# The five written-out queue orders of a one-core hybrid decoder layer, exchanged for another set

## The chip, the cores and the metric

The kernel runs on one core of a Trainium2 chip. The metric is the device time of one execution in microseconds (us), taken as the median of several runs. The core has five instruction queues that matter here: PE (TensorE, the matmuls), DVE (VectorE), ACT (ScalarE), POOL (GpSimd) and SP (SyncE, which only issues transfers; ACT issues some too). Each queue is served in the order in which its instructions stand, and an instruction whose data are not there holds up everything behind it on its queue.

## The reference

One layer of a decoder over 2048 prompt tokens and 8 single-token samples, in 32-bit floats, with width 1024:

```python
xn = _rmsnorm(x, norm1_g)
z = jnp.einsum('btd,de->bte', xn, w_in)
xr, gr, q, k, v = jnp.split(z, IN_SPLITS, axis=-1)
xc, new_conv = _causal_conv(xr, conv_buf, conv_w, conv_b)
hs, h_last = _rglru(xc, h0, gate_a_w, gate_a_b, gate_x_w, gate_x_b, lru_lambda)
rec = (hs * jax.nn.gelu(gr.astype(jnp.float32))).astype(x.dtype)
att = _prompt_attention(q, k, v, attn_sinks)   # window 128, with a sink per head
...
mix = jnp.concatenate([_rmsnorm(rec, rec_norm_g), _rmsnorm(att, attn_norm_g)], axis=-1)
h = x + jnp.einsum('bte,ed->btd', mix, w_out)
hn = _rmsnorm(h, norm2_g)
ff = jax.nn.silu(jnp.einsum('btd,df->btf', hn, w_gate)) * jnp.einsum('btd,df->btf', hn, w_up)
y = h + jnp.einsum('btf,fd->btd', ff, w_down)
```

The inner width of the last part (the FFN) is 2816. The samples use caches of keys and values, and the caches, shifted by one, are outputs too.

## The kernel before

**Numbers in two parts.** Every value that goes into a matmul is split in a high part (a CAST to a shorter 32-bit form, `fp32r`) and a low part (the value minus the high part), and every product is three matmuls: high by high, high by low, low by high (`mm3`, L990). So each weight tile that comes from memory, such as `raw_in` for the input projection, is cast on ACT to a high half (L936), its low half is made on POOL or DVE (L937), and the pair is stored for later use (`split_w`, L955).

**Stages.** Tokens go through the input projection (matmuls `ip`), the recurrence (`rec_chunk`, L1320), the attention (`attn_item`, L1484) and the output projection (`out_unit` and `out_half`, L1623 and L1652) in four groups of 520, 512, 512 and 512 tokens. The FFN then takes three portions of 344 or 342 token columns at a time by two. It uses the seven products of a fast 2x2 block multiplication in place of eight, so the blocks are first added and subtracted: `hn_mix` (L1070) loads parts of the normed stream (`n<-hs`), combines them on DVE (L1082, L1090) and stores the combinations (`mixed<-n`); `hn_load` (L1127) fetches them (`m<-mixed`) and splits them to high and low (ACT L1138; DVE or POOL L1139) as tiles `hn`. `products` (L1914) multiplies them by the gate weights into PSUM tiles `ps_g` and by the up weights into `ps_u`, and copies or adds the banks together in SBUF tiles `c_g` and `c_u` (ACT L1985 and L1990, DVE L1964); `down` (L2003) takes the way back (`pd`, `pw`, and DVE adds to `y`).

**Places where the prediction's steps lie.**

- At the start, 256 KB weight pieces `raw_in` (three buffers), the tokens `xs`, the gate weights `gw` and copies of the two caches (`out_skw`, `out_svw`, L1178 and L1179) all come through SP. `prep_first` (L1228) makes the normed tokens `xn` (L998, L999).
- In the attention, an exponential is turned by PE (`pt`, L968), its high half `pth` is cast on ACT (L1536), its low half `ptl` is made on DVE (L1537), and PE multiplies both by the values (`o`). The recurrence is a scan on DVE (L1376, one instruction per chunk) with two products `rrec` (L1384). `hn_mix` for the first FFN portion runs beside the last attention blocks and has few stage buffers: a load `n<-hs` waits until an older `mixed<-n` store from the same buffer has ended.
- At the entry of the FFN, `out_half` stores the last pieces of the stream from tiles `xres` (`hs<-xres`, L1688, on ACT's queue), while the first gate and up products begin.

**What sets the order.** The program is written as some hundred generators (`x0`, `r33`, `mix0` ...) which a small planner (`Chains`) interleaves. What decides in the end is the table `ORDER` at L104: for each of the five engines one string of runs, `key+pop:count`, where the key is a generator (or for PE a group of matmuls). `order` (L972) takes the instructions in that sequence and links each to the one before it with a dependency that carries no wait, so the string is the order of the queue. Waits for data and buffers are added on top and don't depend on the table.

Of the kernel before, what the change touches and what calls it, by code (L numbers as in the profile page):

```python
# [2259 lines left out]
```

## Time and profile before

| what | value |
|---|---|
| median of 3 runs | 2038.34 us (2037.39 to 2038.42) |
| the profiled execution, its time | 2035.2 us |
| the profiled execution, its span | 2033.4 us |
| PE busy | 2004.7 us (99% of the span), 12273 matmuls |
| DVE busy | 1472.9 us (72%) |
| ACT busy | 955.0 us (47%) |
| POOL busy | 906.8 us (45%) |
| mean granted TensorE clock, by 50 us | 1.00 but for the first, the last and two others |

The span is the time from the first to the last instruction of one execution; the time holds 1.8 us more that lie around it. In the windows view each row is one stretch of the span, with each engine's busy time in it and, in brackets, the number of instructions. In the timeline view a row is an instruction or a run of equal ones: start, duration, engine, line, what it writes and reads, and in square brackets how long the engine had been idle and whose work ended that. In the chain view a row is a start, a duration and what the end of the program was waiting for at that time. An engine name with a q behind it (SPq) is the queue at issue.

### The profile page before, as it was taken

What the parts mean: (1) busy time and instruction counts of PE and PEld (TensorE: products, weight loads), DVE (VectorE), ACT (ScalarE), POOL (GpSimd) and SP (SyncE); (2) the same over time, 40 slices, a digit from 0 to 9 for tenths busy, and PEclk for the clock granted to TensorE, in tenths of its full rate; (3) what the DMA queues carried; (4) which work ended last, traced back from release to release, by engine and by line L of the source; (5) the groups of instructions that cost most, each with busy time, mean ns of one, the idle gap of its engine ahead of it and who ended that gap; (6) DMA issues with size and microseconds to landing.
All of it is one profiled execution on the core that took longest, in us unless ns stands there. A gap on an engine that the chain in (4) does not pass through costs nothing.

```text
span 2033.4 us, 34750 instructions
## 1 busy us (share of the span) xinstructions
PE 2004.7 (99%) x12273; PEld 1904.5 (94%) x12273; DVE 1472.9 (72%) x2694; ACT 955.0 (47%) x1960; POOL 906.8 (45%) x799
## 2 busy tenths in 40 slices
PE   9999999999999999999999999999999999999997
PEld 8988887888778999999999999999999999999997
DVE  6888986777886777765555777787767666776675
ACT  5776764654563543443344533343335433433443
POOL 4312451120132796676666645565557422322333
PEclk9999999999999999999999999999999999999999
DMA  9863675667688776764546687776668675555552
GB/s 338 297 215 127 225 273 182 210 197 223 206 288 272 285 245 208 240 212 168 184 172 224 229 282 242 261 240 214 228 209 290 204 236 196 182 197 199 195 173 101
DMA packets 208991, 450.98 MB, mean 222 GB/s; under 512 B 25232, under 2 KB 82720, under 8 KB 208800
## 3 DMA queue, kind: packets, MB, share of 16 engines
q1 hardware_dynamic: 205184, 445.73, 65.2%
q10 hardware_dynamic: 3632, 3.02, 0.5%
q8 instruction: 97, 1.59, 0.3%
q14 instruction: 78, 0.64, 0.1%
HBM read 335.89 MB, written 113.84 MB: 221 GB/s over the span
## 4 chain that ended last, share of the span: by engine, by line
PE 88%; DMA 6%; DVE 4%; issue 1%; ACT 1%; SPq 0%; DVEq 0%; ACTq 0%
PE ps_g L963 20%; PE ps_u L963 20%; PE ip L963 14%; PE pw L963 12%; PE pd L963 11%; PE op L963 5%; PE s L963 1%; DMA m<-mixed 1%; PE g L963 1%; PE pt L968 1%; PE o L963 1%; DMA mixed<-n 1%; DMA y<-hs 1%; DMA xs<-in_xT 0%; DMA hn<-mixed 0%
## 5 line engine op out<-in xcount | busy, mean ns | idle before, releaser
L963 PE MATMUL ps_g<-hn,w_g 128*128 128x342 f32 (+1 forms) x2772 | 546.0, 320 | 1.8 <-DMA w_g<-split_g 1.0
L963 PE MATMUL ps_u<-hn,w_u 128*128 128x342 f32 (+1 forms) x2772 | 529.8, 320 | 4.5 <-ACT c_u L1985 3.5
L963 PEld LDWEIGHTS ps_u<-hn,w_u 128*128 128x128 f32 x2772 | 455.0, 189 | 5.5 <-ACT c_u L1985 3.8
L963 PEld LDWEIGHTS ps_g<-hn,w_g 128*128 128x128 f32 x2772 | 456.6, 189 | 2.5 <-ACT w_d L1778 2.3
L963 PE MATMUL ip<-xn,w_in 128*128 128x512 f32 (+1 forms) x1680 | 367.3, 361 | 3.9 <-ACT w_in L936 2.7
L963 PEld LDWEIGHTS ip<-xn,w_in 128*128 128x128 f32 x1680 | 271.5, 190 | 49.4 <-issue 4.8
L2050 DVE TENSOR_TENSOR y<-y,pw 128x342 f32<-128x342 f32 x504 | 242.7, 506 | 94.8 <-PE pw L963 90.4
L963 PE MATMUL pd<-fh,w_d 128*128 128x344 f32 (+1 forms) x960 | 235.0, 320 | 0.0
L963 PE MATMUL op<-mix,w_out 128*128 128x512 f32 (+1 forms) x960 | 209.8, 362 | 0.3 <-DVE mix L999 0.3
L2021 DVE TENSOR_TENSOR y<-y,pd 128x344 f32<-128x344 f32 (+1 forms) x240 | 119.6, 509 | 103.3 <-PE pd L963 91.1
L963 PEld LDWEIGHTS op<-mix,w_out 128*128 128x128 f32 x960 | 157.6, 190 | 30.0 <-issue 6.1
L963 PE MATMUL pw<-fh,wd 128*128 128x342 f32 x576 | 167.5, 319 | 1.0 <-DVE y L2021 1.0
L963 PEld LDWEIGHTS pd<-fh,w_d 128*128 128x128 f32 x960 | 167.3, 188 | 0.0
L963 PE MATMUL pw<-t,wd 128*128 128x342 f32 x648 | 150.6, 319 | 0.0
L963 PE MATMUL pd<-fl,w_d 128*128 128x344 f32 (+1 forms) x480 | 147.6, 320 | 0.0
L1946 POOL TENSOR_TENSOR c_u<-c_u,c_g 128x342 f32<-128x342 f32 (+1 forms) x60 | 58.8, 980 | 180.2 <-DVE c_u L1964 144.5
L1964 DVE TENSOR_TENSOR c_u<-c_u,ps_u 128x342 f32<-128x342 f32 (+1 forms) x99 | 50.5, 510 | 122.1 <-PE ps_u L963 121.8
L1935 DVE TENSOR_TENSOR fl<-c_u,fh 128x342 fp32r<-128x342 f32 (+1 forms) x132 | 118.5, 909 | 15.3 <-ACT fh L1934 14.2
L1779 POOL TENSOR_TENSOR w_u<-ru,w_u 128x512 fp32r<-128x512 f32 x44 | 58.9, 1340 | 151.8 <-ACT w_u L1778 123.0
L1934 ACT CAST fh<-c_u 128x342 fp32r<-128x342 f32 (+1 forms) x132 | 62.1, 479 | 106.4 <-POOL c_u L1946 41.9
L963 PEld LDWEIGHTS pw<-t,wd 128*128 128x128 f32 x648 | 111.4, 189 | 0.0
L963 PEld LDWEIGHTS pw<-fh,wd 128*128 128x128 f32 x576 | 105.6, 189 | 1.3 <-DVE y L2021 1.3
(299 smaller groups left out, 3499.9 us busy)
## 6 DMA issues: line engine op xcount, KB each, us to landing
w_g<-split_g SPq DMA_DIRECT2D x88, 512.0 KB, 4.4
w_u<-split_u SPq DMA_DIRECT2D x88, 512.0 KB, 5.5
w_in<-split_w SPq DMA_DIRECT2D x84, 512.0 KB, 3.6
rg<-in_wgate SPq DMA_DIRECT2D x110, 256.0 KB, 3.1
ru<-in_wup SPq DMA_DIRECT2D x110, 256.0 KB, 3.3
w_out<-split_w SPq DMA_DIRECT2D x48, 512.0 KB, 4.8
split_g<-w_g SPq DMA_DIRECT2D x44, 512.0 KB, 2.8
split_u<-w_u SPq DMA_DIRECT2D x44, 512.0 KB, 2.9
```

What stands on the lines that cost most here:

```text
L963: r = nc.tensor.matmul(*args, **kw)
L968: r = nc.tensor.transpose(*args)
L1779: lo_eng.tensor_tensor(w[:, 1, :], src, w[:, 0, :].bitcast(F32), op=ALU.subtract)
L1934: nc.scalar.copy(hi, v)
L1935: nc.vector.tensor_tensor(lo, v, hi.bitcast(F32), ALU.subtract)
L1946: (nc.vector if p == NPAIR - 1 or src is not v else eng(E_MUL[2 * h + n])).tensor_tensor(v, src, g, op=ALU.mult)
L1964: nc.vector.tensor_tensor(o, a, b, op)
L2021: nc.vector.tensor_tensor(ys[gi, n, m], ys[gi, n, m], ps, ALU.add)
L2050: nc.vector.tensor_tensor(v, v, ps, ALU.add)
```

## The change

Only the five strings of `ORDER` differ. They hold the same instructions of every engine (12043 entries for PE, 2566 for DVE, 1815 for ACT, 795 for POOL, 1416 for SP) in another order, found by a planner which takes it that VectorE and GpSimd never work at the same time. Constants, tiles, buffers, engines of each operation and waits for data stay. The table is longer by 61 lines, so every line number of the code behind it is higher by 61 (L963 becomes L1024). Core of the diff, the first line of PE's and of SP's string:

```diff
 ORDER = {
     "PE": """
-w_st_x0:17 ip0_1_0 ip0_1_1 ip0_12_1 ip0_12_0 ip0_1_0:2 ip0_1_1:2 ip0_1_0 ip0_12_1 ip0_1_1 ip0_12_0:2 ip0_12_1 ip0_12_0
+w_st_x0:17 ip0_1_0 ip0_1_1 ip0_12_1 ip0_12_0 ip0_1_1 ip0_12_1 ip0_1_1 ip0_1_0 ip0_12_0 ip0_1_0:2 ip0_1_1 ip0_12_0
...
     "SP": """
-x0:9 x0+1 x0+1 x0+1 pro+1 pro x0 r01 pro v0 q02 xs1:2 cache:2 v0+1 r01 k0 q02 k0+1 v0 r00 v0 xs1:2 r00+1 k0 r03 k0
+x0:9 x0+1 x0+1 x0 v0 x0 pro xs1 r01 v0+1 xs1 r01 cache pro+1 q02 k0 q02 k0+1 cache v0 pro r00 v0 cache r00+1 r03 xs1
```

Of the entries, 53% keep their place on PE, 30% on DVE, 47% on ACT, 63% on POOL and 37% on SP; the others move by a few places, and in the steady part of the FFN whole groups move further (the loads and sums of `hn_mix` for the second and third portion by up to 91 places on SP and 148 on DVE).

**SP, the start.** The first twelve transfers that follow the tokens, before:

```order
L1239 DMA cs<-in_cst 128x384
L1185 DMA gw<-in_gatew 128x1024
L1184 DMA scv<-in_sconv 128x96
L931 DMA raw_in_12_1_185<-in_win 128x512
L955 DMA split_w<-w_in_1_0_166 128x1024
L1186 DMA sh<-in_sh 128x32
L931 DMA raw_in_9_0_368<-in_win 128x512
L955 DMA split_w<-w_in_12_0_171 128x1024
L1292 DMA xt_0_1418<-in_xR 128x512
L1292 DMA xt_1_1421<-in_xR 128x512
L1178 DMA out_skw<-in_ck 8x16256
L1179 DMA out_svw<-in_cv 8x16256
```

and after:

```order
L992 DMA raw_in_12_1_185<-in_win 128x512
L992 DMA raw_in_9_0_368<-in_win 128x512
L1300 DMA cs<-in_cst 128x384
L1245 DMA scv<-in_sconv 128x96
L1353 DMA xt_0_1418<-in_xR 128x512
L1016 DMA split_w<-w_in_1_0_166 128x1024
L992 DMA raw_in_9_1_374<-in_win 128x512
L1353 DMA xt_1_1421<-in_xR 128x512
L1016 DMA split_w<-w_in_1_1_180 128x1024
L1239 DMA out_skw<-in_ck 8x16256
L1247 DMA sh<-in_sh 128x32
L1016 DMA split_w<-w_in_12_0_171 128x1024
```

`raw_in_9_1` stood behind all twelve of the first list, and is seventh now. Two pieces of `raw_in` go first, and `gw`, `sh`, `xt_1`, one of the two stores `split_w` and both cache copies (`out_skw`, `out_svw`) come behind `raw_in_9_1`.

**DVE, near the end of the attention.** The scans of the last recurrence chunks (`q<-..,carry,ix`), the two products `rrec`, softmax steps (`sc`), an addition to the stream (`xres`) and the three steps of `hn_mix` on tiles `n_3_0` and `n_3_1`, before:

```order
L1376 SCALAR_TENSOR_TENSOR q_1_5902<-a_2_5901,carry,ix_2_5899 128x512
L1376 SCALAR_TENSOR_TENSOR q_1_5902<-ia_3_5945,carry,ix_3_5952 128x512
L1384 SCALAR_TENSOR_TENSOR rrec<-rrec,q_1_5902 128x512 x2
L1526 TENSOR_SCALAR sc_0_6723<-sc_0_6723,mx_0_6724 128x256 x2
L1638 TENSOR_TENSOR xres_5_6137<-xres_5_6137,op_5_0_6188 128x512
L1082 SCALAR_TENSOR_TENSOR n_3_1_5510<-n_3_1_5510,vec,hb_1_5363 128x344
L1082 SCALAR_TENSOR_TENSOR n_3_0_5513<-n_3_0_5513,vec,hb_0_5356 128x344
L1090 TENSOR_TENSOR n_3_1_5510<-n_3_1_5510,n_3_0_5513 128x344
L1537 TENSOR_TENSOR ptl_1_0_6701<-pt_1_0_6695,pth_1_0_6700 128x512
```

and after:

```order
L1699 TENSOR_TENSOR xres_5_6137<-xres_5_6137,op_5_0_6188 128x512
L1143 SCALAR_TENSOR_TENSOR n_3_0_5513<-n_3_0_5513,vec,hb_0_5356 128x344
L1143 SCALAR_TENSOR_TENSOR n_3_1_5510<-n_3_1_5510,vec,hb_1_5363 128x344
L1151 TENSOR_TENSOR n_3_1_5510<-n_3_1_5510,n_3_0_5513 128x344
L1587 TENSOR_SCALAR sc_0_6723<-sc_0_6723,mx_0_6724 128x256
L1437 SCALAR_TENSOR_TENSOR q_1_5902<-ia_3_5945,carry,ix_3_5952 128x512
L1445 SCALAR_TENSOR_TENSOR rrec<-rrec,q_1_5902 128x512
L1587 TENSOR_SCALAR sc_0_6723<-sc_0_6723,mx_0_6724 128x256
L1445 SCALAR_TENSOR_TENSOR rrec<-rrec,q_1_5902 128x512
L1598 TENSOR_TENSOR ptl_1_0_6701<-pt_1_0_6695,pth_1_0_6700 128x512
```

The three `n` steps stood behind the second scan and both products; they stand ahead of them now, and the product and scan rows come behind whatever those steps wait for.

**ACT and PE, the entry of the FFN.** ACT's queue around the copy that empties the first bank of the up product (`c_u_0_10<-ps_u_0_1`), before:

```order
L1943 ACT_TABLE_LOAD
L1943 ACTIVATE c_g_0_00_7116<-c_g_0_00_7116 128x344
L1688 DMA hs<-xres_4_6798 128x512
L1138 CAST hn_1_8_7715<-m_4_0_7714 128x344
L1778 CAST w_u_0_7_7886<-s_u_0_7884 128x512
L1138 CAST hn_1_8_7715<-m_4_1_7719 128x344
L1985 COPY c_u_0_10_7130<-ps_u_0_1_7909 128x344
L1943 ACTIVATE c_g_0_11_7119<-c_g_0_11_7119 128x344
L1138 CAST hn_1_9_7720<-m_4_2_7724 128x344
```

and after:

```order
L1749 DMA hs<-xres_4_6798 128x512
L1199 CAST hn_1_8_7715<-m_4_0_7714 128x344
L1199 CAST hn_1_8_7715<-m_4_1_7719 128x344
L2004 ACT_TABLE_LOAD
L2004 ACTIVATE c_g_0_00_7116<-c_g_0_00_7116 128x344
L1839 CAST w_u_0_3_7905<-s_u_0_7903 128x512
L1199 CAST hn_1_9_7720<-m_4_2_7724 128x344
L1839 CAST w_u_0_5_7866<-s_u_0_7844 128x512
L2004 ACTIVATE c_g_0_11_7119<-c_g_0_11_7119 128x344
L2004 ACTIVATE c_g_0_01_7117<-c_g_0_01_7117 128x344
L2046 COPY c_u_0_10_7130<-ps_u_0_1_7909 128x344
```

The store `hs<-xres_4` was behind a load of a function table and one activation, and is ahead of both now; the copy to `c_u_0_10`, which was fourth behind that store, is tenth now. On PE, the last rows ahead of the first matmuls of `w_u_0_6`, which write the bank that this copy empties, and these themselves, before:

```order
L963 MATMUL ps_g_0_1_7771<-hn_1_8_7715,w_g_0_4_7785 128x344 x2
L963 MATMUL ps_g_0_5_7822<-hn_1_7_7706,w_g_0_3_7767 128x344
L963 MATMUL ps_g_0_1_7771<-hn_1_8_7715,w_g_0_4_7785 128x344
L963 MATMUL ps_g_0_5_7822<-hn_1_7_7706,w_g_0_3_7767 128x344
L963 MATMUL ps_u_0_1_7909<-hn_0_5_6377,w_u_0_6_7862 128x344 x3
```

and after:

```order
L1024 MATMUL ps_u_0_2_7926<-hn_0_2_6231,w_u_0_2_7819 128x344
L1024 MATMUL ps_u_0_2_7926<-hn_0_3_6282,w_u_0_2_7819 128x344 x2
L1024 MATMUL ps_g_0_1_7771<-hn_1_8_7715,w_g_0_4_7785 128x344
L1024 MATMUL ps_g_0_1_7771<-hn_1_9_7720,w_g_0_4_7785 128x344
L1024 MATMUL ps_u_0_2_7926<-hn_0_3_6282,w_u_0_2_7819 128x344
L1024 MATMUL ps_u_0_2_7926<-hn_0_4_6372,w_u_0_2_7819 128x344 x2
L1024 MATMUL ps_g_0_1_7771<-hn_1_8_7715,w_g_0_4_7785 128x344
L1024 MATMUL ps_u_0_2_7926<-hn_0_4_6372,w_u_0_2_7819 128x344 x2
L1024 MATMUL ps_u_0_2_7926<-hn_0_5_6377,w_u_0_2_7819 128x344
L1024 MATMUL ps_u_0_2_7926<-hn_0_4_6372,w_u_0_2_7819 128x344
L1024 MATMUL ps_g_0_1_7771<-hn_1_9_7720,w_g_0_4_7785 128x344
L1024 MATMUL ps_u_0_1_7909<-hn_0_5_6377,w_u_0_6_7862 128x344 x3
```

The first `w_u_0_6` matmuls came straight behind the `ps_g_0_5` ones; now twelve of `w_u_0_2` into another bank, and three more into `ps_g_0_1`, come first.

More of the change, by code (lines that the diff above doesn't have):

```diff
@@ new lines @@
+ip0_10_1:18 ip0_13_0 ip0_10_1:2 ip0_13_0:2 ip0_10_1 ip0_13_0:19 ip0_13_1 ip0_13_0 ip0_13_1:3 ip0_13_0 ip0_13_1:16
+ip0_2_0 ip0_13_1:2 ip0_2_0:2 ip0_13_1 ip0_2_0 ip0_13_1 ip0_2_0:5 s0_0_0:4 ip0_2_0:2 s0_0_1 ip0_2_0:2 s0_0_1:2
+ip0_2_0:7 s0_0_1 ip0_2_0:3 ip0_2_1:3 ip0_2_0 ip0_2_1:3 ip0_5_0 ip0_2_1:6 s0_1_0:4 s0_1_1:4 ip0_2_1:8 s1_0_0 ip0_2_1
+s1_0_0 ip0_2_1 s1_0_0:2 ip0_2_1 pt0_0_1 ip0_2_1 pt0_0_1 s1_0_1:2 pt0_0_1 s1_0_1 ip0_5_0 s1_0_1 ip0_5_0 pt0_0_1
+ip0_5_0:17 ip0_5_1 ip0_5_0 o0_0_0 ip0_5_0:3 ip0_5_1:3 s1_1_0:3 ip0_5_1:4 s1_1_0 ip0_5_1 pt0_1_1 ip0_5_1 pt0_1_1:2
@@ new lines @@
+op0_2_260 s6_1_1 op0_2_260:11 op0_3_0:4 o5_0_1 op0_3_0:12 g1_2_0_0 op0_3_0:4 pt5_1_0 op0_3_0 pt5_1_0 op0_3_0:2 pt5_1_0
+op0_3_0 op0_3_260:3 o5_0_1 op0_3_260:2 pt5_1_0 op0_3_260:18 op0_4_0 op0_3_260 op0_4_0:15 g1_2_1_0 op0_4_0:7
+op0_4_260:2 op0_4_0 op0_4_260:15 o5_1_0 op0_4_260:5 pt5_1_1 op0_4_260 pt5_1_1:2 op0_4_260 pt5_1_1 op0_5_0 o5_1_0
+op0_5_0:13 o5_1_1 op0_5_0:6 op0_5_260:3 op0_5_0:3 op0_5_260:2 op0_5_0 op0_5_260:5 s7_0_0 op0_5_260 s7_0_0:2
+op0_5_260:4 s7_0_0 op0_5_260:2 pt6_0_0:3 op0_5_260 o5_1_1 pt6_0_0 op0_5_260 s7_0_1:4 op0_5_260 op0_6_0 op0_5_260:2
@@ new lines @@
+d1_10_0_1:6 d1_10_1_1:2 d1_10_2_1 d1_10_1_1:3 d1_10_2_1:3 d1_10_3_1 d1_10_2_1 d1_10_3_1:2 d1_10_4_1 d1_10_3_1
+d1_10_4_1 d1_10_3_1:2 d1_10_5_1:2 d1_10_4_1:4 d1_10_5_1:4 g2_0_5 d1_10_7_1 d1_10_6_1:3 d1_10_7_1 d1_10_6_1 d1_10_7_1
+d1_10_6_1:2 d1_10_7_1:2 d1_10_0_0:2 d1_10_7_1 d1_10_0_0:2 d1_10_1_0:2 d1_10_0_0:2 d1_10_1_0 d1_10_2_0 d1_10_1_0:2
+d1_10_2_0 d1_10_1_0 d1_10_2_0:3 d1_10_3_0 d1_10_2_0 d1_10_3_0:4 d1_10_4_0:4 d1_10_3_0 d1_10_4_0:2 d1_10_6_0
+d1_10_5_0:5 d1_10_6_0:5 d1_10_7_0:2 d1_10_5_0 d1_10_7_0:3 g2_0_5:3 d1_10_7_0 g2_0_5:6 g2_0_7 g2_0_5 g2_0_7 g2_0_5
@@ new lines @@
+d2_10_0_1 d2_10_1_1 d2_10_0_1 d2_10_1_1 d2_10_0_1:2 d2_10_1_1 d2_10_2_1 d2_10_1_1 d2_10_2_1:2 d2_10_1_1 d2_10_2_1
+d2_10_3_1 d2_10_4_1 d2_10_2_1 d2_10_3_1:4 d2_10_4_1:2 d2_10_3_1 d2_10_4_1 d2_10_5_1 d2_10_4_1:2 d2_10_5_1:4 d2_10_6_1
+d2_10_5_1 d2_10_6_1:5 d2_10_7_1:2 d2_10_0_0 d2_10_7_1:4 d2_10_0_0:5 d2_10_1_0:6 d2_10_2_0:3 st_f2_1:3 d2_10_2_0:3
+d2_10_3_0:6 d2_10_4_0:3 d2_10_5_0 d2_10_4_0:3 d2_10_5_0:5 d2_10_6_0:5 d2_10_7_0 d2_10_6_0 bc_f2_1 w_st_f2_0
+d2_10_7_0:2 w_st_f2_0 d2_10_7_0:3 w_st_f2_0 bc_f2_1 w_st_f2_0:6 bc_f2_1 w_bc_f2_0:3 st_f2_0:6 bc_f2_0:3
@@ L686 @@
+wd2.10 wd2.10+1 wd2.10 f21:3 f20:8
 """,
     "SP": """
-x0:9 x0+1 x0+1 x0+1 pro+1 pro x0 r01 pro v0 q02 xs1:2 cache:2 v0+1 r01 k0 q02 k0+1 v0 r00 v0 xs1:2 r00+1 k0 r03 k0
-r03+1 r00 xs1:2 q01 r00 q01+1 r03 q00 r03 xs1:2 q00+1 q01 q03 q01 q03+1 x1 q00 x1 r02 q00 r02+1 q03 x1 g01 q03 x1
-g01+1 r02 g00 r02 x1:2 g00+1 g01:2 g02 x1 g00 k1 g02+1 g03 x1 k1 g00 g02 g03+1 xs2 v1 g02 v1 xs2:2 o00 cache g03 o00+1
-q10:2 g03 o01 xs2 q11 dec:2 q11 g10 xs2:2 g10 r10:2 xs2 o00+2 q12 xs2 q12 q13 x2:2 q13 r11:2 g11:2 r12:2 g12:2 o01+3
@@ L746 @@
+wg2.9+4 wu2.9 wg2.9 wd2.8 wg2.9 wd2.8 wg2.9 wu2.9 wg2.9 wd2.8 wg2.10 wu2.9+4 wd2.9 wg2.10 wd2.9+1 wd2.9 wu2.9 wd2.9:2
+wu2.9:3 wu2.10 wg2.10+4 wg2.10 wd2.9 wg2.10 wd2.9 wg2.10:2 wu2.10 wd2.9 wd2.10:2 wu2.10+4 wd2.10 wu2.10 wd2.10
+wu2.10:3 f21:8 f20:4
 """,
```

1294 lines of the change are left out of this document (667 added, 627 removed).

## Prediction

> **What bounds the kernel now.** I read the page's head first, then the busy time by 50 us, then what PE waits for, and then the rows at the three places where it waits longest. From the page:
>
> ```profile
> span 2033.4 us, 34750 instructions
> PE 2004.7 (99%) x12273; PEld 1904.5 (94%) x12273; DVE 1472.9 (72%) x2694; ACT 955.0 (47%) x1960; POOL 906.8 (45%) x799
> PE 88%; DMA 6%; DVE 4%; issue 1%; ACT 1%; SPq 0%; DVEq 0%; ACTq 0%
> ```
>
> PE is busy for 2004.7 of 2033.4 us, so all that any order of the same instructions can win is the other 28.7 us; the chain that ends last is PE's for 88%. Where those 28.7 us lie is in the windows view (a stretch; then busy us of each engine in it, with the number of instructions):
>
> ```profile
> 0.00:50.00 50.00, 45.09 (x337) 43.98 (x338) 32.64 (x69) 28.82 (x57) 23.77 (x30) 0.97 0.93 338
> 500.00:550.00 50.00, 50.00 (x241) 40.43 (x240) 44.78 (x88) 28.63 (x56) 9.66 (x12) 1.00 0.67 210
> 550.00:600.00 50.00, 47.64 (x226) 37.75 (x224) 42.69 (x97) 32.53 (x67) 14.58 (x15) 1.00 0.83 268
> 600.00:650.00 50.00, 47.13 (x215) 37.97 (x216) 33.01 (x57) 20.35 (x41) 10.76 (x8) 0.93 0.79 259
> 650.00:700.00 50.00, 46.35 (x264) 43.65 (x263) 35.99 (x50) 26.91 (x55) 33.78 (x24) 0.97 0.91 329
> 700.00:750.00 50.00, 50.00 (x320) 49.75 (x318) 37.40 (x46) 23.93 (x46) 48.38 (x34) 1.00 0.68 230
> 1150.00:1200.00 50.00, 48.14 (x317) 47.59 (x317) 34.70 (x57) 14.92 (x30) 19.95 (x17) 1.00 0.78 262
> 2000.00:2050.00 50.00, 23.08 (x158) 22.71 (x156) 21.00 (x45) 12.41 (x25) 11.44 (x12) 0.90 0.17 57
> ```
>
> 4.9 us are lost in the first 50, 8.9 us from 550 to 700 (2.4, 2.9 and 3.7), 1.9 us around 1175, and at the end PE has 23.08 of the 33.4 us that are left, so 10.3 us. The rest of the span has 2.7 us between them. A steady stretch of the FFN (700 to 750) has 320 matmuls in 50 us, which is 156 ns each, without a gap. What ended PE's idle times:
>
> ```profile
> PE pt L968 <- DVE ptl L1537: 4.4, 4, 2.1
> PE ps_u L963 <- ACT c_u L1985: 3.5, 1, 3.5
> PE ip L963 <- ACT w_in L936: 2.7, 3, 1.6
> PE bc_f L963 <- DVE cols_f L2103: 1.8, 1, 1.8
> ```
>
> The sum, the times and the longest, in us. The first three lie at the places whose order is shown above: the attention's end, the FFN's entry and the start. The fourth is in the last norm, whose order stays.
>
> **The start: -2.1 us.** The longest `w_in` wait, on ACT's queue (of 1.65 us for PE by its own timeline), and the chain ahead of it:
>
> ```profile
> 25.25 0.62 PE L963 MATMUL ip<-xn,w_in 128*128 128x260 f32 x3 [1.65 <-ACT w_in L936]
> 24.58 0.62 ACT L936 CAST w_in<-raw_in 128x512 fp32r<-128x512 f32 x1 [2.76 <-DMA raw_in<-in_win]
> 15.93 8.55 DMA raw_in<-in_win
> DMA packets 6597, 15.24 MB, mean 339 GB/s; under 512 B 1249, under 2 KB 1377, under 8 KB 6577
> 15.29 8.32 PE L963 MATMUL ip<-xn,w_in 128*128 128x260 f32 x67 [0.44 <-ACT w_in L936]
> ```
>
> The cast at 24.58 waits for `raw_in_9_1`, issued at 15.93 and 8.55 us under way, with all transfers together at 339 GB/s. In the new order `gw` (512 KB), two cache copies (508 KB each), a `split_w` store (512 KB), `xt_1` (256 KB) and `sh` (16 KB) come behind it: 2312 KB, which at 339 GB/s is 7.0 us. PE needs only 1.65 us of that, so this wait should go; so should the one of 0.44 us at 15.29, whose `raw_in_12_1` is now the first of the list. Together -2.1. What is late next: `gw` feeds the gate matmuls, which the new PE order brings 26 to 219 places forward, and the first of these is not held up by `gw` but by `xc`:
>
> ```profile
> 43.31 0.60 PE L963 MATMUL g<-xc,gw 128*128 128x260 f32 x2
> 37.53 2.85 DVE L1338 SCALAR_TENSOR_TENSOR xc<-xr,vec,xc 128x512 f32<-128x512 f32 x2
> 36.06 0.75 DVE L1338 SCALAR_TENSOR_TENSOR xc<-xr,vec,xc 128x512 f32<-128x512 f32 x1 [0.29 <-ACT xc L1333]
> ```
>
> `xc` is complete at 40.4, and 26 places of 156 ns or less take the first `g` from 43.3 to about 39.2 us; but the waits that vanish bring `xc` forward with everything else by 2 us. A new wait of up to 1 us is the other bound. Range of this term: -2.1 to +1.
>
> **The attention's end: +1.5 us.** PE waits for `ptl` here, and `ptl` stands on DVE's queue behind the three `hn_mix` steps. DVE's rows, and the chain that leads to them:
>
> ```profile
> 586.87 2.24 DVE L1376 TENSOR_TENSOR_SCAN q<-ia,carry,ix 128x512 f32<-128x512 f32 x1
> 589.04 1.26 DVE L1384 SCALAR_TENSOR_TENSOR rrec<-rrec,q 128x512 f32<-128x512 f32 x2
> 590.22 0.60 DVE L1526 TENSOR_SCALAR sc<-sc,mx 128x256 f32<-128x256 f32 x2
> 593.72 1.74 DVE L1082 SCALAR_TENSOR_TENSOR n<-n,vec,hb 128x344 f32<-128x344 f32 x2 [2.30 <-DMA n<-hs]
> 595.50 0.52 DVE L1090 TENSOR_TENSOR n<-n,n 128x344 f32<-128x344 f32 x1
> 584.10 5.45 DMA mixed<-n
> 589.56 4.14 DMA n<-hs
> ```
>
> The step at 593.72 waits for a load of 4.14 us, which waits for a store of 5.45 us out of the same stage buffer. This pair of transfers, not DVE, sets when the three steps can run. Before, the scan (2.24), both `rrec` (1.26) and two `sc` (0.60) ran while the load was under way, and 2.30 us of idle time were left. Now they stand behind the three steps: 4.1 us of work moves from inside the wait to behind it. If the load lands when it did, all of it comes on top: +4.1. But the steps of the pairs before stand 2 to 5 places further forward too, so store and load begin earlier by some of it. At the best the transfers move forward by as much as the steps do, the wait of DVE is not longer than before, and PE's wait of 2.1 us goes: -2.1. Between these I take that the load lands about 2.6 us earlier, by five places of 0.5 us (the 0.52 of the row above), which leaves 4.1 - 2.6 = +1.5.
>
> The new planner holds DVE and POOL apart, and the trace shows that this is worth something only for some operations:
>
> ```profile
> L2050 DVE TENSOR_TENSOR y<-y,pw 128x342 f32<-128x342 f32 x504 | 242.7, 506 | 94.8 <-PE pw L963 90.4
> L1935 DVE TENSOR_TENSOR fl<-c_u,fh 128x342 fp32r<-128x342 f32 (+1 forms) x132 | 118.5, 909 | 15.3 <-ACT fh L1934 14.2
> 593.32 1.28 POOL L1010 TENSOR_TENSOR hacc<-hacc,sq_h 128x512 f32<-128x512 f32 x1
> ```
>
> Equal shapes: 506 ns where one input is in PSUM (`pw`), 909 ns on the mean where both are in SBUF. And of the two `n` steps at 593.72, which took 1.74 us, the first met the POOL row at 593.32; at the 0.75 us of the `xc` row, of the same kind with half as many columns again, two would take 1.5 at most. So to hold the two apart gives 0.2 us or somewhat more here, not the 2.3 us that the load costs. [...]
>
> **The entry of the FFN: -2.5 us.**
>
> ```profile
> 680.45 1.25 PE L963 MATMUL ps_u<-hn,w_u 128*128 128x344 f32 x4 [3.55 <-ACT c_u L1985]
> 673.86 0.35 ACTq L1688 DMA_DIRECT2D hs<-xres  x1
> 671.88 1.28 ACT L1943 ACT_TABLE_LOAD   x1
> 679.96 0.45 ACT L1985 COPY c_u<-ps_u 128x344 f32<-128x344 f32 x1 [4.18 <-DMA m<-mixed]
> 673.88 6.09 DMA m<-mixed
> ```
>
> PE waits 3.55 us for the copy that empties `ps_u_0_1`, and the copy waits 4.18 us for a transfer. The views name an `m<-mixed` load of 673.88; the copy neither reads nor writes `m`, and the `hs<-xres` store was issued within 0.02 us of it, so I take it that the copy's buffer lies where `xres` lay, and waits for that store. In the new order PE has 15 more matmuls ahead of the first that needs the bank: 15 x 156 ns = 2.3 us of cover. And the store goes ahead of the table load (1.28) and an activation, so the copy can begin up to 1.8 us earlier. Both together could clear 3.55. But six rows more stand between store and copy on ACT, one of them the cast of a load `m_4_2`, one an activation whose sum comes late; I give back about 1 us for these: -2.5. Bounds: all of it, -3.5, and nothing, 0, where the cast waits for its load as long as the copy did.
>
> **The steady FFN: 0.** The sums of `hn_mix` for the second and third portion move up by up to 148 places on DVE and 91 on SP, and weight loads go back by up to 41. PE's 50.00 of 50 with 37.40 on DVE covers it; without cover, a weight load that is late by one store (5.45, as above) would cost up to that. **The small waits: -0.3.** Two more matmuls of 156 ns stand ahead of two of the short waits at the turns between portions. The 10.3 us of the end and the wait for `cols_f` stay.
>
> **Sum.** -2.1 + 1.5 - 2.5 - 0.3 = -3.4 us on the profiled execution of 2035.2 (span 2033.4), so 2031.8. That execution lies 3.1 us under the median of 2038.34, and the change is carried over: 2038.34 - 3.4 = 2034.9 us.
>
> **The rivals.** About 0.2% (4.1 us) is what a measurement of this kernel can tell from no change: faster is below 2034.3, slower above 2042.4.
>
> 1. *The attention's end gains too.* The steps further forward pull the store and load forward with them, and PE's wait there goes: -2.1 - 2.1 - 3.5 - 0.3 = -8.0, 2030.3. For it: the transfers are the chain there, and each starts when a step ends. Against it: 5.45 + 4.14 us for each pair leave little for DVE's order to say. The planner's premise would give it as well, if DVE and POOL excluded each other in all operations: POOL's 14.58 us between 550 and 600 then lie in DVE's way, and to move them out is worth the 2.1. The row of 506 ns speaks against that.
> 2. *Slower: the attention's end loses all of it.* The load lands where it did, +4.1, and scans, `rrec` and `ptl` come later by that. It decides where the `n<-hs` load ends after about 593 us, as it did at 593.70. If the copy at the FFN's entry then waits too (0), and the start gains half (-1) or loses 1, it is +3.1 to +5.1: 2041.4 to 2043.4.
> 3. *Nothing that can be measured.* PE is full; what is won at the start is caught up by the chain of transfers that leads to the attention's end, and the next wait takes the place of the last: -1 to +1, 2037.3 to 2039.3.
>
> **How the numbers follow.** The forecast's mechanism (start and entry gain, attention's end loses a little) gets 0.43, with its own range of -6 to -1 (2032.3 to 2037.3); rival 1 gets 0.2, rival 2 0.18, rival 3 0.19. Faster by over 0.2%: all of rival 1 and nearly half of the forecast, 0.2 + 0.2 = 0.40. Slower: two thirds of rival 2, 0.12, and 0.03 for a late weight load in the steady FFN, 0.15. Within: the rest, 0.45. The range takes in rival 1 and 1 us below it, since the small waits may go too, and of rival 2 the near end: 2029.0 to 2041.5.
>
> **What would show it.** In the profile after: PE's busy time in the first 50 us up from 45.09 to about 47.2, and no `w_in` wait of 1.6; the DVE idle time ahead of the `n` steps near 590 longer than 2.30, and the `ptl` waits longer than 4.4 in sum; the `c_u` wait of 3.5 down to about 1. The prediction is wrong if the 4.1 us behind the `n` steps turn up nowhere, if `c_u` still waits 3 us or more, or if a steady FFN stretch loses PE time to a weight load.

## The result: 17 us faster, and where it came from

The changed kernel takes 2020.97 us (median of 4 runs, 2018.78 to 2022.32), the kernel before in the same runs 2038.12 (2037.39 to 2038.42). The ratio is 0.9915 with a 95% interval of 0.9898 to 0.9933, so 17 us less (14 to 21). Only fast executions are compared; one of the kernel before took 3284 us at a granted clock of 0.56 and is left out. The forecast was 2034.9, 3.4 us less, with a range from 2029.0: it gave a gain over 0.2% a chance of 0.40 and no measurable change 0.45, the gain is five times the forecast, and the range was missed. Rival 1, which let the attention's end gain too, gave 2030.3 and is missed as well.

The page of the changed kernel's profiled execution (2018.78 us):

```profile
span 2017.0 us, 34720 instructions
PE 1999.7 (99%) x12273; PEld 1899.3 (94%) x12273; DVE 1460.9 (72%) x2694; ACT 952.2 (47%) x1960; POOL 907.1 (45%) x799
PE 90%; DVE 5%; DMA 2%; issue 1%; ACT 1%; POOL 1%; SPq 0%; ACTq 0%; DVEq 0%; POOLq 0%
```

The span is 16.4 us shorter. PE's idle time went from 28.7 to 2017.0 - 1999.7 = 17.3 us, which is 11.4. The other 5.0 are in PE's busy time, 2004.7 to 1999.7 us for the same 12273 matmuls. The prediction had no term for that: the work itself ran faster. The windows, the same stretches as before:

```profile
0.00:50.00 50.00, 47.37 (x362) 45.86 (x362) 35.64 (x78) 32.30 (x64) 26.80 (x30) 1.00 0.92 327
550.00:600.00 50.00, 49.42 (x240) 39.02 (x239) 43.64 (x97) 33.80 (x73) 15.73 (x17) 1.00 0.87 290
600.00:650.00 50.00, 49.47 (x239) 40.07 (x238) 34.64 (x57) 20.68 (x41) 12.81 (x10) 1.00 0.89 292
650.00:700.00 50.00, 48.90 (x299) 47.40 (x299) 40.10 (x49) 28.97 (x60) 41.43 (x31) 1.00 0.93 324
700.00:750.00 50.00, 49.34 (x316) 49.05 (x315) 42.75 (x57) 21.20 (x42) 43.78 (x31) 1.00 0.75 253
1150.00:1200.00 50.00, 50.00 (x328) 49.99 (x327) 37.19 (x67) 16.77 (x34) 26.15 (x24) 1.00 0.86 290
```

The column behind the engines is the granted TensorE clock. It is 1.00 in all of these; before it was 0.97, 0.93 and 0.97 in the first, third and fourth. The longest wait that is left, some of the shorter ones, and what remains of the wait for `ptl`:

```profile
PE bc_f L1024 <- DVE cols_f L2164: 2.5, 1, 2.5
PE st_x L1024 <- DVE epsc L975: 1.0, 1, 1.0
PE ip L1024 <- ACT xn L1059: 1.0, 1, 1.0
PE ps_g L1024 <- ACT hn L1199: 0.7, 1, 0.7
PE pt L1029 <- DVE ptl L1598: 0.2, 1, 0.2
```

The three large waits of before (4.4 for `ptl`, 3.5 for `c_u`, 2.7 for `w_in`) are gone, and the one in the last norm is 0.7 longer. To put the gain in places, I gave every matmul of both traces the usual start-to-start time of its width, added these up in order of time, and compared when each kernel has reached the same sum. The changed kernel is ahead by 1.9 us before the attention's end (before's 535 us), by 7.7 behind it (617 us), by 12.1 behind the FFN's entry (705 us), by 11.5 to 1000 us, by 14.6 behind the first turn between portions (1210 us), by 16.5 behind the second (1582 us), and by 16.0 at the end. So: start -1.9, attention's end -5.8, entry -4.4 with 0.6 given back behind it, turns -5.0, end +0.5.

These shares come from one execution of each kernel. The other traces of this record hold each stretch in one order or the other, and the same sums over them (the kernels with repeated matmuls or shortened sums left out) tell which shares are the order's. With the new order, the attention's end (535 to 652 us) takes 6.1 to 7.0 us less than in this execution of the kernel before; with the old one, from 2.2 less to 0.6 more. The first turn (1085 to 1210 us) takes 2.4 to 3.1 less with the new order, and 0.1 to 1.0 more with the old. At the second turn (1300 to 1582 us) every trace with the new order has 2.0 less, but of the eight others with the old order four have 1.9 or 2.0 less too: the waits at 1330 and 1562 us come and go in the old order, and most of this share can't be put down to the change. Nor is the start's share steady: in a second profiled execution of the changed kernel some 2.5 us of lead at 29 us had gone at 535.

### The profile page after: what moved, and what is told of

Same layout as the page of the kernel before. It is cut to its first block, busy times and chain, and to the rows that moved or that the text cites. A ratio compares the mean times of both kernels' runs of the same rounds, so it can differ in the third digit from the quotient of the medians.

```text
span 2017.0 us, 34720 instructions
## 1 busy us (share of the span) xinstructions
PE 1999.7 (99%) x12273; PEld 1899.3 (94%) x12273; DVE 1460.9 (72%) x2694; ACT 952.2 (47%) x1960; POOL 907.1 (45%) x799
## 4 chain that ended last, share of the span: by engine, by line
PE 90%; DVE 5%; DMA 2%; issue 1%; ACT 1%; POOL 1%; SPq 0%; ACTq 0%; DVEq 0%; POOLq 0%
PE ps_u L1024 21%; PE ps_g L1024 21%; PE pw L1024 12%; PE pd L1024 11%; PE ip L1024 11%; PE op L1024 8%; DMA raw_in<-in_win 2%; PE s L1024 1%; PE o L1024 1%; PE pt L1029 1%; PE g L1024 1%; DVE sc L1587 0%; POOL w_in L998 0%; DVE sc L1576 0%; DVE xc L1399 0%
## 5 line engine op out<-in xcount | busy, mean ns | idle before, releaser
L1024 PE MATMUL ps_g<-hn,w_g 128*128 128x342 f32 (+1 forms) x2772 | 565.4, 320 | 1.8 <-ACT hn L1199 0.7
L1024 PE MATMUL ps_u<-hn,w_u 128*128 128x342 f32 (+1 forms) x2772 | 547.6, 319 | 0.0
L1024 PEld LDWEIGHTS ps_g<-hn,w_g 128*128 128x128 f32 x2772 | 460.3, 188 | 2.9 <-ACT hn L1199 1.0
L1024 PEld LDWEIGHTS ps_u<-hn,w_u 128*128 128x128 f32 x2772 | 457.7, 188 | 0.1
L1024 PE MATMUL ip<-xn,w_in 128*128 128x512 f32 (+1 forms) x1680 | 369.7, 360 | 1.8 <-ACT xn L1059 1.0
L1024 PEld LDWEIGHTS ip<-xn,w_in 128*128 128x128 f32 x1680 | 269.6, 188 | 46.4 <-issue 4.1
L1024 PE MATMUL pd<-fh,w_d 128*128 128x344 f32 (+1 forms) x960 | 234.4, 320 | 0.0
L1024 PE MATMUL op<-mix,w_out 128*128 128x512 f32 (+1 forms) x960 | 211.4, 361 | 0.2 <-DVE xres L1699 0.2
L1024 PEld LDWEIGHTS op<-mix,w_out 128*128 128x128 f32 x960 | 156.6, 188 | 29.5 <-issue 5.5
L1024 PE MATMUL pw<-fh,wd 128*128 128x342 f32 x576 | 171.6, 319 | 0.0
L1024 PEld LDWEIGHTS pd<-fh,w_d 128*128 128x128 f32 x960 | 167.3, 188 | 0.0
L1024 PE MATMUL pw<-t,wd 128*128 128x342 f32 x648 | 160.9, 319 | 0.0
L1024 PE MATMUL pd<-fl,w_d 128*128 128x344 f32 (+1 forms) x480 | 145.2, 320 | 0.0
L1996 DVE TENSOR_TENSOR fl<-c_u,fh 128x342 fp32r<-128x342 f32 (+1 forms) x132 | 105.9, 810 | 18.0 <-ACT fh L1995 15.6
L1024 PEld LDWEIGHTS pw<-t,wd 128*128 128x128 f32 x648 | 113.3, 189 | 0.0
L1840 POOL TENSOR_TENSOR w_d<-rd,w_d 128x512 fp32r<-128x512 f32 x60 | 86.0, 1444 | 53.7 <-ACT w_d L1839 48.1
```

Of the source, the lines that this page charges most:

```text
L1024: r = nc.tensor.matmul(*args, **kw)
L1840: lo_eng.tensor_tensor(w[:, 1, :], src, w[:, 0, :].bitcast(F32), op=ALU.subtract)
L1996: nc.vector.tensor_tensor(lo, v, hi.bitcast(F32), ALU.subtract)
```

## The experiments

Each kernel is spliced out of the two tables. An instruction belongs to a part of the program by the time at which it started in the profile of the kernel whose order is used there; the rest follow in the other order. A time in brackets is the interval of the ratio of the times, turned into us with 2036 us. Single executions of the kernel before lay between 2031 and 2043 us on the chips of these runs, so the difference that one such kernel makes is known to some 2 us.

**By places.** Four kernels use the new order in one part each:

```diff
-ORDER: old
+r1_start: new to 112 us, then old
+r2_attn: old to 545 us, new to 645 us, then old
+r3_entry: old to 653 us, new to 794 us, then old
+r4_turns: old to 855 us, then new
```

> All five queues in the new order for what ran in the first 112 us, the rest in the old order. Theory (each place gains by itself, as the same amount of PE work is reached earlier or later in the two traces): 1.5 to 2 us under the kernel before, with PE's busy time in the first 50 us near 47.4 instead of 45.1. Rival (the lead is used up by the chain of transfers at the attention's end, which starts when the last recurrence chunk is done): within 0.5 us of the kernel before.

> All five queues in the new order only for what runs from 545 to 650 us (the attention's end and the output projection behind it), the rest in the old order. Theory: about 5.8 us under the kernel before, of which 2.8 are waits of PE that vanish and 3.0 a granted clock that no longer falls to 0.5 between 610 and 616 us. Rival (the gain there needs the earlier start, which lets the loads of the mix steps begin earlier): 0 to 2 us, with the clock still low behind the waits.

> All five queues in the new order only for what runs from 653 to 794 us (the entry of the FFN), the rest in the old order. Theory: about 4.2 us under the kernel before: 3.6 of waiting for the copy of the first up product, 1.7 of a granted clock that no longer falls to 0.5 between 681 and 685 us, less 1.1 of short waits that are new. Rival (the wait only moves, since the store and the loads under way there are as many as before): less than 1.5 us under.

> All five queues in the new order for what runs behind 855 us, the old order before it. Theory (the mix steps of the second and third portion run earlier, in the quiet part of the FFN, and leave SP and the transfers free for the weights at the turns between portions): 4 to 5 us under the kernel before, and the waits near 1112, 1183, 1199, 1330 and 1562 us gone. Rival (these waits vanish in the changed kernel because its portions begin 12 us earlier against the transfers that were started before them): less than 1.5 us under.

| new order in | ratio | us |
|---|---|---|
| start | 0.9991 | -1.8 (-3.9 to +0.2) |
| attention's end | 0.9964 | -7.3 (-10.2 to -4.7) |
| FFN's entry | 0.9988 | -2.4 (-4.5 to -0.4) |
| all behind 855 us | 1.0023 | +4.7 (+2.2 to +6.9) |

The attention's end gained by itself what the trace had shown (5.8 lies within its interval). The start's time agrees with its trace, though its interval just takes in no gain at all. The FFN's entry, at -2.4, lies between its theory (4.2) and its rival (under 1.5): in its trace it is 5.1 us ahead behind the copy of the first up product, by equal PE work, and 3.7 of that are given back up to 755 us. The kernel with the new order behind 855 us was slower, against both expectations; its profile shows why:

```profile
PE ps_u L1003 <- DVE c_u L2004: 5.7, 1, 5.7
```

This is one wait at the seam. What the new order had begun before 855 us, the mix steps of the second portion above all, came at once behind it, and by equal PE work 8.7 us were lost there: 5.7 are the wait, and 3.0 come behind it, where the granted clock is 0.65 from 865 to 870 us and 0.67 from 870 to 875. Behind the seam the kernel won 4.4 back at the turns.

> The old order for what runs before 653 us, the new one for all that is behind it, so that no seam lies within the FFN. The seam at 855 us cost its kernel 8.7 us, since the mix steps of the second portion, which the new order begins before that time, all came at once behind it; behind the seam 4.4 us were gained at the turns. Theory: entry -4.2, turns -4.5, end +0.6: about 8 us under the kernel before. Rival (the seam's loss belongs to the new order itself, which trades the steady part for the turns): under 4 us.

```diff
-ORDER: old
+r5_ffn: old to 653 us, then new
```

This came out at 0.9972, -5.7 us (-7.7 to -3.7), between the two theories. In its profile no wait at the turns is left, and it is ahead by 5.6 us behind the copy of the first up product (by equal PE work); of that, 3.7 are given back up to 755 us, 4.1 won at the turns, and 1.2 lost again at the end. The seams have a price of their own, so the parts are not exact: -1.8, -7.3 and -5.7 make -14.8 for a whole of -17.3.

**The attention's end, in pieces.**

```diff
-r2_attn: new from 545 to 645 us on all queues
+r6_mix_only: there, only the first mix steps at their new places, on DVE and SP
+r7_no_mix: there, all but the first mix steps in the new order
+r9_attn_old_pe: there, all queues but PE in the new order
+r10_attn_old_sp: there, all queues but SP in the new order
```

> The old order everywhere, but in the part from 545 to 650 us the steps of the first mix (their loads, products, sums and stores, on VectorE and SyncE alone) stand at the places that they have in the new order. Theory (each step further forward releases a stage buffer earlier, so store and next load begin earlier, and the last pair of loads lands 8 us earlier): most of the 5.8 us of this part, so 4 to 6 us under the kernel before, with VectorE's wait for the last load near 594 us under 1 us. Rival (the gain is in the order of the attention's own instructions on the five queues): less than 1.5 us under, VectorE's wait for the load still 2 us or longer.

> The counterpart: the new order for what runs from 545 to 650 us on all five queues, but the steps of the first mix at the places that they have in the old order. Theory: 0 to 2 us under the kernel before, with the waits for the low halves of the transposed softmax still there. Rival (the attention's own order gives the gain): 4 to 6 us under.

> As the kernel with the new order from 545 to 650 us on all queues, but PE's queue in the old order there. The mix steps alone gave nothing and the rest alone cost time, so the part works only as a whole; this asks whether PE's own order is in it. Theory (what counts is that VectorE, ScalarE and SyncE agree on when the mix steps run, PE only waits less): 5 to 7 us under the kernel before, as with all queues. Rival (PE's new order covers the waits with matmuls of the output projection): 0 to 3 us under, with the waits for the low halves back over 2 us in sum.

> As the kernel with the new order from 545 to 650 us on all queues, but the queue that issues the transfers (SyncE) in the old order there. Theory (steps done earlier must also be stored earlier and the next load issued earlier): most of the gain goes, 0 to 3 us under the kernel before, and VectorE waits 2 us or longer for the last loads of the mix steps. Rival (SyncE is idle most of the time and its order is of no weight): 5 to 7 us under.

The mix steps alone: 1.0009, +1.8 us (-0.4 to +4.1). All but them: 1.0013, +2.6 (+0.8 to +4.7). All queues but PE: 0.9969, -6.3 (-8.8 to -3.9). All queues but SP: 1.0040, +8.1 (+5.5 to +10.8). My theory at that time, that earlier mix steps make the gain, fell with the first of these, and its rival, that the attention's own order makes it, with the second. The issue of the last pair of loads `n<-hs` on SP's queue shows what happens, in the kernel before, with the mix steps alone, and in the changed kernel:

```profile
589.56 0.80 SPq L1080 DMA_DIRECT2D n<-hs  x2
```

```profile
586.99 0.91 SPq L1080 DMA_DIRECT2D n<-hs  x2
```

```profile
581.26 0.93 SPq L1141 DMA_DIRECT2D n<-hs  x2
```

The mix steps alone bring the loads forward by 2.6 us, which is what the prediction had estimated, and the whole change by 8.3, of which some 1.8 are the lead from the start (in the kernel with the new order here alone they go out at 583.11, so 6.5 earlier). With SP in its old order, VectorE stands before transfers that this queue issues too late:

```profile
580.45 0.69 DVE L1641 TENSOR_TENSOR xres<-xres,op 128x512 f32<-128x512 f32 x1 [4.64 <-DMA xres<-in_xT]
598.23 0.69 DVE L1641 TENSOR_TENSOR xres<-xres,op 128x512 f32<-128x512 f32 x1 [2.73 <-DMA xres<-in_xT]
601.72 0.58 DVE L1085 SCALAR_TENSOR_TENSOR n<-n,vec,hb 128x344 f32<-128x344 f32 x1 [2.81 <-DMA n<-hs]
```

So VectorE's new order needs SP's: the loads of `xres` and of `n` share the queue, and each is needed at the place where the new VectorE order has put its user. PE's own order adds nothing that these runs can tell.

**The granted clock.** The kernel before shows it in steps of 5 us around the two waits:

```profile
605.00:610.00 5.00, 2.71 (x17) 1.77 (x15) 5.00 (x9) 2.91 (x7) 1.27 (x1) 0.91 0.85 279
610.00:615.00 5.00, 4.67 (x13) 3.72 (x14) 4.42 (x10) 3.44 (x7) 1.52 (x1) 0.50 0.48 138
675.00:680.00 5.00, 1.91 (x13) 1.62 (x11) 2.83 (x4) 0.78 (x3) 4.33 (x3) 1.00 0.99 321
680.00:685.00 5.00, 4.55 (x19) 4.55 (x20) 0.94 (x2) 2.96 (x7) 2.49 (x3) 0.66 1.03 408
```

The column behind the five engines is the clock. PE is busy for 2.71 of 5 us and the clock falls to 0.50 in the five that follow; it is busy for 1.91, and the next five have 0.66. To tell a consequence of standing still from any other cause, one kernel repeats matmuls in the waits:

```diff
+REPEAT = {("op2_7_0", 5): 10, ("o15_0_1", 0): 9, ("g0_0_4", 2): 22}
...
             issued.setdefault(key, []).append(r)
+            n = REPEAT.get((key, len(issued[key]) - 1), 0)
+            for _ in range(n):
+                issued.setdefault("rep_" + key, []).append(nc.tensor.matmul(*args, **kw))
             return r
```

> The old order, with matmuls repeated where PE would wait anyway: ten of an output projection before the first long wait for the low halves near 594 us, four and five of an attention product near 606 and 609 us, and 22 of a gate product before the wait for the copy of the first up product at 677 us. What they add twice changes the output. They cost about 2.1, 0.9, 1.1 and 3.4 us of PE, as long as the waits are. Theory (the granted clock falls because PE stood still, and PE's work behind the wait is then slower): no clock under 0.9 from 600 to 690 us, and 3.0 + 1.7 us less behind the waits: 3 to 5 us under the kernel before. Rival (the clock falls for another reason, such as the traffic of the transfers or the mixture of the instructions): the same clock rows as before, and the time within 1 us of before or later.

0.9980, so -4.1 us (-6.5 to -1.8) with 41 matmuls more. The same rows of its profile:

```profile
605.00:610.00 5.00, 4.50 (x26) 3.39 (x24) 3.83 (x8) 3.32 (x7) 1.78 (x2) 1.00 0.91 294
610.00:615.00 5.00, 4.64 (x28) 3.81 (x28) 5.00 (x9) 3.44 (x7) 2.42 (x2) 1.00 0.62 190
675.00:680.00 5.00, 5.00 (x32) 4.74 (x31) 2.61 (x4) 0.52 (x2) 4.39 (x3) 1.00 0.98 338
680.00:685.00 5.00, 4.37 (x28) 4.34 (x28) 0.94 (x2) 3.00 (x7) 2.28 (x2) 1.00 1.04 410
```

The clock stays at 1.00, with as much traffic as before in the last row (410 GB/s for 408). It is not the luck of one execution: the mean granted clock of the twelve timed executions is 0.995 to 0.997, against 0.992 to 0.997 for 35 of the kernel before on the same chip, on average 0.997 against 0.994, and in the changed kernel it is 0.997 to 0.998. At these two places the fall of the clock is caused by PE standing still: with the waits filled it is 1.00 in every step of 2 us from 600 to 618 us and from 676 to 688, where the kernel before has 0.50 from 610 to 614 and from 682 to 684. Work that is thrown away made the old order faster by about as much as its waits cost behind themselves (3.0 and 1.7 us by the trace).

**VectorE and GpSimd apart.** In two kernels GpSimd's sums of squares in this part touch 8 columns and not 512, so that they hardly last.

```diff
+SHORT = {"rc3_1", "rc3_2", "rc3_3"} | {f"h2_{m}" for m in range(8)}
...
-                return (eng or nc.gpsimd).tensor_tensor(acc[:, :T], acc[:, :T], sq[:, :T], op=ALU.add)
+                n = 8 if name in SHORT else T
+                return (eng or nc.gpsimd).tensor_tensor(acc[:, :n], acc[:, :n], sq[:, :n], op=ALU.add)
```

> The old order on all queues, with GpSimd's sums of squares over the third token group's stream and the fourth group's recurrence cut from 512 to 8 columns, which leaves out most of these two sums, so that GpSimd hardly works beside VectorE between 560 and 610 us. Theory (what VectorE loses there to GpSimd, about 1 us on the scan, 0.7 on a mix step and 1 on a softmax step, lies within its waits for the loads of the mix steps): within 1.5 us of the kernel before, with the longest wait for the low halves still near 2 us. Rival (the collisions of VectorE and GpSimd make the waits at the attention's end, so an order that keeps them apart gains by that): 3 to 6 us under, with the low clock behind the waits gone.

> The new order on all queues, with the same sums of squares on GpSimd cut from 512 to 8 columns as in the kernel of the old order with short sums, which leaves out most of these two sums. There the cut gave 2.7 us (0.8 to 4.7). Theory (the new order already keeps GpSimd's sums off the VectorE steps that PE waits for): within 1.5 us of the changed kernel. Rival (the new order gains by other things, and the collisions are still paid): 2 us or more under the changed kernel.

> The changed kernel itself, on the same chip as the two others of this call, as what the short sums are compared with. Both theories: 0.99 of the kernel before, as it was timed first.

In the old order the cut gives 0.9987, -2.6 us (-4.7 to -0.8), neither of the two expectations. In the new order it gives nothing: 0.9918 beside 0.9915 for the changed kernel timed with it (2020.09 and 2019.95 us). So what the two engines cost each other on PE's path in the old order is no longer paid in the new one. Set against the -7.3 of this part, the 2.6 are about a third; that the new order's gain holds just these 2.6 is an estimate from the two intervals, not a measurement. In the old order the scan and the wait behind it were, with the sums cut:

```profile
585.95 1.26 DVE L1378 TENSOR_TENSOR_SCAN q<-ia,carry,ix 128x512 f32<-128x512 f32 x1
592.85 0.58 DVE L1084 SCALAR_TENSOR_TENSOR n<-n,vec,hb 128x344 f32<-128x344 f32 x1 [2.29 <-DMA n<-hs]
```

and in the changed kernel, with the whole sums:

```profile
588.47 1.28 DVE L1437 TENSOR_TENSOR_SCAN q<-ia,carry,ix 128x512 f32<-128x512 f32 x1
586.67 1.07 DVE L1143 SCALAR_TENSOR_TENSOR n<-n,vec,hb 128x344 f32<-128x344 f32 x2
```

The scan had taken 2.24 us beside GpSimd. Without it VectorE is done sooner, but the wait for the load stays as long as it was (2.29 for 2.30); only the changed kernel has no wait there. The two engines still meet in the changed kernel: from 582.58 us a sum on GpSimd runs beside the other scan, which had begun at 582.49. There the scan takes 1.27 us, and the sum 2.27 instead of the 1.28 of its equals at 593.89 and 595.91.

**The turns between portions.** Two complementary kernels:

```diff
-ORDER: old
+r12_before_turn: old to 653 us, new to 1040 us, then old
+r13_from_turn: old to 1085 us, then new
```

> The old order before 653 us, the new one up to 1040 us of the changed kernel's time (the first portion of the FFN with the mix steps of the second), the old one for all behind that, so both turns stand in the old order. Theory (the mix steps that run early are what clears the first turn): entry -4 and first turn about -2, so 4 to 6 us under the kernel before, without the waits near 1112, 1183 and 1199 us. Rival (the order within the turn clears it): the waits at the first turn as before, and 2 to 4 us under.

> The complement of the kernel that keeps both turns in the old order: the old order up to 1085 us, the new one behind it. Theory (the order within the turns clears their waits: transfers for the next portion start some 10 us earlier and are spread): the waits near 1112, 1183, 1199, 1330 and 1562 us gone, behind them 4 to 5 us less than before, and of this a seam at 1085 us may take back a part, since what the new order has begun before it comes at once. Rival (it needs the mix steps that run early in the first portion): the waits at the first turn as before.

The first is at 0.9983, -3.5 us (-5.1 to -1.6), which is the entry's share, and it waits at the first turn where the kernel before did, some 4.5 us earlier (two of the three waits are ended by other work than before):

```profile
1107.72 0.55 PE L975 MATMUL ps_g<-hn,w_g 128*128 128x342 f32 x2 [0.85 <-ACT fh L1946]
1178.69 0.71 PE L975 MATMUL ps_u<-hn,w_u 128*128 128x342 f32 x3 [0.66 <-ACT w_g L1790]
1194.73 0.42 PE L975 MATMUL pw<-fh,wd 128*128 128x342 f32 x1 [1.16 <-DVE y L2033]
```

In the second none of the five waits of before is left in the trace, and it is at 0.9982, -3.7 us (-5.7 to -1.6). What runs in the quiet part is not what clears the first turn; the order from the turn on does. For the second turn the pair shows nothing, since the waits at 1330 and 1562 us are missing from both traces. The "10 us earlier" of my expectation was misread: the changed kernel is 11 us ahead there with all it does, and in this kernel, which has no such lead, the transfers of the turn begin no earlier than before. What differs is seen in steps of 10 us (DMA share and GB/s are the last columns), first of the kernel before, then of the one with the new order from the turn on:

```profile
1160.00:1170.00 10.00, 10.00 (x72) 9.99 (x72) 9.49 (x11) 4.20 (x9) 8.03 (x8) 1.00 0.23 80
1180.00:1190.00 10.00, 9.18 (x59) 8.93 (x58) 6.29 (x13) 1.06 (x2) 1.19 (x1) 1.00 0.93 296
1190.00:1200.00 10.00, 8.96 (x57) 8.68 (x57) 4.49 (x10) 3.75 (x7) 4.06 (x3) 1.00 1.01 365
```

```profile
1160.00:1170.00 10.00, 10.00 (x74) 9.99 (x74) 7.54 (x12) 4.24 (x9) 7.61 (x6) 1.00 0.73 230
1180.00:1190.00 10.00, 10.00 (x66) 10.00 (x65) 9.14 (x18) 1.07 (x2) 1.19 (x1) 1.00 1.02 354
1190.00:1200.00 10.00, 10.00 (x66) 10.00 (x65) 3.31 (x7) 3.75 (x7) 4.55 (x4) 1.00 0.95 317
```

The old order lets the transfers fall to 80 GB/s shortly before PE waits for a weight at 1183 and for an addition behind a load at 1199; the new one moves 230 GB/s at that time, and PE is full. In the kernel with the old order at the turns the same hollow stands 4.5 us earlier (87 and 71 GB/s from 1155.5 to 1165.5 us), so it belongs to the order. That the hollow is what makes the two waits is argued from this, and no run changes SP's order alone at this place. For the wait at 1112 us no such row was found, and which of the queues clears it stays open.

No spliced kernel beats the changed one.

## Why the prediction was wrong, point by point

- **The start (forecast -2.1): right in what it named, and its size agrees.** PE's busy time in the first 50 us went to 47.37, where about 47.2 was expected, and the long `w_in` wait is gone. By equal PE work the lead is 3.7 us at 29 us, and 1.9 of it last in this execution, nothing in another; the new order in the start alone measures -1.8 (-3.9 to +0.2).
- **The attention's end (forecast +1.5): wrong in sign; this is the step that failed.** The step read: "Between these I take that the load lands about 2.6 us earlier, by five places of 0.5 us (the 0.52 of the row above), which leaves 4.1 - 2.6 = +1.5." For the mix steps alone it holds in the trace (2.6 us, of which that execution had some 0.6 before this part), and the time of that kernel, +1.8 (-0.4 to +4.1), is in keeping with it. But the change moves 120 instructions of VectorE in this part, 73 of SP and 64 of ACT, and I costed three of them as if the others stood. With the whole change the loads go out 8.3 us earlier and no wait for them is left. Rival 1 named that outcome, for the reason that the transfers are the chain; its reason against ("leave little for DVE's order to say") was mistaken, since SP's order was changed with it, and without SP's the part loses 8.1.
- **The clock: a term that was missing (-5.0).** The prediction said that all an order can win is PE's idle 28.7 us. Its own rows had 0.93 and 0.97 in the column of the clock. In steps of 2 us the trace of the kernel before shows what they stand for: at the FFN's entry 3.55 us without work and then 0.50 from 682 to 684 us, and at the attention's end, where no wait is longer than 2.1 us, 0.50 from 610 to 614 us. The filled waits show that these waits were paid for a second time: about 3 us behind those near 605 us and 1.7 behind the one that ended at 680, by equal PE work.
- **VectorE and GpSimd (0.2 us or somewhat more): too small.** Short sums gave 2.6 (0.8 to 4.7). I had compared two `n` steps, and not the scan (2.24 for 1.26 us); and the two `n` steps take 1.07 us in the changed kernel, so 0.7 were lost there, not the 0.2 taken from the `xc` row. For the additions `y<-y,pw`, with one input in PSUM, the trace of the kernel before shows no loss to GpSimd: 157 of the 504 lie to nine tenths or more beside its instructions and take 505 ns on the mean, 266 meet none and take 507. Of the `fl<-c_u,fh` rows of the same width, both inputs in SBUF, 26 of each kind take 1102 and 507 ns. In the changed kernel the mean of the 504 is as it was:

```profile
L2111 DVE TENSOR_TENSOR y<-y,pw 128x342 f32<-128x342 f32 x504 | 241.4, 505 | 98.5 <-PE pw L1024 93.6
```

  So the planner's premise was too strict for these additions. No loss from that is seen: between 760 and 1085 us, where PE has no wait over 0.25 us in either kernel, the lead stays as it is.
- **The FFN's entry (forecast -2.5): right mechanism; its size lies between 2.4 and 4.4.** In the changed kernel's trace the whole wait of 3.5 us went, and the 1.7 of the clock with it; 0.7 and a few shorter waits are new. The new order at this place alone measures -2.4 (-4.5 to -0.4), with the first portion behind it -3.5. I gave back 1 us for rows that stand between store and copy; in the changed kernel ACT comes to the copy without a wait, 5.8 us behind the store:

```profile
662.82 0.33 ACTq L1749 DMA_DIRECT2D hs<-xres  x1
668.66 0.42 ACT L2046 COPY c_u<-ps_u 128x344 f32<-128x344 f32 x1
```

  That the copy waits for this store, and not for the load that the views name, was argued from 0.02 us. The landings in the traces bear it out: in all ten kernels with the old order at this place and in the one with repeated matmuls, the copy begins 0.17 to 0.23 us after the store has landed (before: 679.78 and 679.96 us), and in nine of them the load `m<-mixed` lands only after the copy has begun (before: 680.10).
- **The turns (forecast -0.3): too small by about 3 at the first turn.** The difference in the two traces is 5.0, but of the 1.9 at the second turn most can't be put down to the order. I counted the matmuls that stand ahead of each wait, and took the rest of the order there as it was; the new order issues transfers in a stretch that the old one left almost empty (80 GB/s between 1160 and 1170 us). For the steady part between, 0 was right.
- **The end (forecast 0): +0.5**, the wait for `cols_f` of 2.5 for 1.8.

## What to carry to other kernels

When a table moves everything in a part of the program, costing the few moved instructions at the critical wait as if the rest stood is not a forecast of the part: look at the chain of transfers that feeds it, and at the queue that issues them, and ask when that chain can begin. Where PE's long waits are, read the granted clock in steps of a few microseconds behind them, and add what it costs (3.0 and 1.7 us here) to the prize of removing the wait; where a wait can't be removed, spare matmuls in it may pay (41 of them gave 4.1 us here). And where the transfers are nearly idle just before PE waits for one, look at the order of their issue before that of the matmuls that wait. Before a gain is put down to a place, look at that place in several executions: two of the five waits at the turns come and go without any change.

## What the runs showed of the hardware that was not expected

In the kernel before, the granted TensorE clock was 0.50 from 680.8 to 684.2 us, behind PE's wait of 3.55 us, and from 609.1 to 615.9, from the beginning of the third of three waits of 0.50, 0.92 and 1.19 us within 5 us; it was 1.00 again about 3.7 and 5.6 us after PE had resumed. The one wait of 2.1 us by itself was not followed by a fall (1.00 from 600 to 605 us), and the changed kernel, whose longest wait before the last norm is 1.0, shows 1.00 from 550 to 750 us. At the copy of the first up product a wait of 4.2 us (the old order with short sums) went with 0.71 and 0.61 in the two steps of 5 us from 675, one of 3.0 (the new order at the attention's end alone) with 0.83 in both from 670, one of 2.5 (the mix steps alone) with 0.71 from 680 to 685, and one of 2.7 (all queues but PE) with 1.00 from 670 to 690, so of the last two the longer wait was the one without a fall. VectorE's second scan took 2.24 us in the kernel before, beside a GpSimd sum that had begun 0.63 us earlier, and 1.26 with the sums cut; in the changed kernel, where the other scan had begun 0.09 us before a sum, the scan took 1.27 and the sum 2.27. The additions `y<-y,pw`, with one operand in PSUM, took 506 ns on the mean in the kernel before and 505 in the changed one.
